# A hybrid decoder block on one core: another order of half-block products, a merge by quarters, a fixed ACT order in the FFN pairs and interleaved w_out tiles

## Chip, cores, metric

The kernel runs on one core of a Trainium2 chip. The metric is the device time of one execution in microseconds (us). Engines are named as the profile names them: PE is TensorE's matmul queue, PEld its weight loads, DVE is VectorE, ACT is ScalarE, POOL is GpSimd, SP is the queue that issues most DMAs.

## What is computed

The reference is one decoder block of width 1024 over a sequence of 1024 tokens: a Mamba-2 mixer and an RG-LRU mixer side by side, gated and merged, then a SwiGLU FFN of hidden width 2816.

```
hn = rmsnorm(h, norm1_w)
gates, z, xbc, dt, lru_x, lru_y = split(hn @ w_in)
gates = sigmoid(gates + b_branch_gate);  g_ssm, g_lru = split(gates)
y_ssm = mamba2_mixer(z, xbc, dt, ...) @ w_out_ssm
y_lru = rglru_mixer(lru_x, lru_y, ...) @ w_out_lru
h = h + (g_ssm * y_ssm + g_lru * y_lru) @ w_out
hn = rmsnorm(h, norm2_w)
gate, up = split(hn @ w_ffn_in)
h = h + (silu(gate) * up) @ w_ffn_out
return rmsnorm(h, norm_f_w)
```

## The kernel before

All data are fp32. A matrix product is made of three passes: every operand is split into a high part (a cast on ACT, L98) and a low part (a subtraction on DVE, L99), and `product` (L905 to L907) issues hi·hi, low weight·hi and hi weight·low activation for every 128 × 128 block of weights against 512 columns. In the trace a cast reads as `whi<-raw` or `xph<-xr`, its low part as `wlo` or `xpl`.

In order of time of the profiled execution: the input projections with the SSM scan (to about 770 us), the RG-LRU (to 1043), two stages for w_out_ssm (1043 to 1212), a short direct part and a third stage for w_out_lru (to 1319), w_out (to 1416), the FFN's 22 pairs (to 1927), two stages for w_ffn_out (to about 2080) and the rest with the last norm.

**Seven products.** Each of the stages is a call of `seven`: a 2 × 2 block product by seven half-size products N1 to N7 instead of eight. Its plan is a table of slots: `at(slot, f, ...)` enters weight loads, activation loads (`load_xop`), casts (`x_part`, `w_part`), weight sums (`w_sum`, on POOL: L959, L962) and products, and the events of a slot are written out in turn. Every N takes two slots, g = 0 and 1, of two products of 12 matmuls each. Before, the order is N2, N5, N3, N1, N6, N7, N4, with one bank for each of the four pairs of rows p that is carried from N2 on. The weights of (0,1), which N2 needs, come into the `raw` tile of the weight pool; the others come into `wr` units. s1 is the sum of (1,0) and (1,1), N5's weight.

**Merge.** The third stage calls `merged` after each product. After N6 the whole tile d, after N7 and N4 halves, are merged: yo = (gate + 1) · yo (L1077), res = res + yo (L1078), both on DVE, and then the halves are cast for w_out (`act_pair`, tiles `un`).

**w_out.** 16 tiles, two halves of the columns by eight row blocks d, in the order of `wo_order` (L136). After a tile of the second half with d of 4 to 7 one half tile of `bn` is cast (b22); after d of 0 to 3, `t_parts` makes four differences on DVE (L1165 to L1168) and casts two units `xth`, `xtl`.

**FFN pairs.** `first_pair` and 21 calls of `pair` make gate and up for 128 columns of hidden width by seven products: a11·b11, s1·t1, s2·t2, a12·b21, s3·t3, s4·b22, a22·t4. ACT copies banks out after the first three (L1259, L1262, L1265). The products with s2 and s3 share one bank. Between the products the next pair is made ready: loads of its two weight tiles `raw`, the split of the first (`whi`, `wlo`), four sums on POOL (L1145 to L1148, in place in `raw`), the split of s1 (`ws1h`) and of both `raw` tiles (`wsh`, `wsl`). `finish_pair` scales, applies Silu (L1214) and stores. In 8 of the pairs `pump` also makes the differences `tu` of finished tiles for w_ffn_out.

The Tile scheduler sets each engine's order by its own estimate of when things are ready, unless `pin` ties an instruction to the one pinned before it on the same engine. All loads and stores go through SP's one queue.

Of the kernel before, what the change touches and what calls it, by code (L numbers as in the profile page):

```python
# [67 lines left out]
def hybrid_block(ctx, tc, xT, w_in, w_dt, w_os, w_ol, w_o, w_fi, w_fo, w_fl, lru_w, params, heads, out):  # L68
# [10 lines left out]
    def store(dst, src):  # L79
        nc.sync.dma_start(out=dst, in_=src)  # L80
# [14 lines left out]

    def split(hi, lo, src):

        S.copy(hi, src)  # L98
        V.tensor_tensor(lo, src, hi.bitcast(F32), op=ALU.subtract)  # L99

    def split_scaled(hi, lo, src, col):

# [30 lines left out]
    order += [PJ_GATE + i for i in range(16 - last_gates, 16)]  # L133
    wseq = [(w_in[f], KD) for f in order]
    wseq_in = len(wseq)
    wo_order = [list(range(KD)), [4, 5, 6, 7, 0, 1, 2, 3]]  # L136
    wseq += [(w_o[d], KD) for h in range(2) for d in wo_order[h]]
    wseq_out = len(wseq)
    wready = []
# [172 lines left out]
    with ExitStack() as st1:  # L312
# [474 lines left out]
        with tc.tile_pool(name="lru", bufs=1, reuse_waits="tile", side="right") as lp, tc.tile_pool(  # L787
# [66 lines left out]
            def gate_done(i):  # L854
                def done(ps):
                    gt = lp.tile([P, T], F32, name="gl")
                    S.activation(gt, ps, AF.Tanh, bias=hgb[:, i : i + 1], scale=0.5)
                    store(gate_d[i], gt)

                return done  # L860

# [12 lines left out]
    def bank():  # L874
        return pb.tile([P, H], F32, name="pbk", tag="pbk")
# [44 lines left out]
    def seven(c0_, act, tdf, w_of, out, pools=None, xpool=None, swap=False, done=None):  # L922


        pools = pools or {}
        wr, wop, xr_, xop, banks = {}, {}, {}, {}, [None] * 4

        def load_w(q, kh, g):

            if (q, kh) == (0, 1):  # L930
                t_ = wpool.tile([P, KD, P], F32, name="raw", tag="raw", bufs=2)
                t_ = t_.rearrange("p (a k) c -> p a k c", a=2)
            else:
                t_ = unit(pools.get((q, kh), ar), F32, "wr").rearrange("p a (k c) -> p a k c", c=P)
            for a in range(2):
                load(t_[:, a], w_of(q * 4 + 2 * g + a, kh))
            wr[q, kh, g] = t_

        def load_xop(n, kk):

            u = unit(xpool if xpool and n == N2 else ar, F32, "xr")
            src, o, h = {
                N2: (act, 4, 0), N5: (tdf, 0, 0), N3: (act, 4, 1), N1: (act, 0, 0),
                N6: (tdf, 4, 1), N7: (tdf, 0, 1), N4: (tdf, 4, 0),
            }[n]
            if swap and src is act:
                h = 1 - h
            for a in range(2):
                load(u[:, a], src[o + 2 * kk + a][:, hcol[h]])
            xr_[n, kk] = u  # L950

        def x_part(n, kk):
            hi, lo = (unit(xpool if xpool and n == N2 else ar, name=x) for x in ("xph", "xpl"))
            split(row(hi), row(lo), row(xr_.pop((n, kk))))
            xop.setdefault(n, []).extend((hi[:, a], lo[:, a]) for a in range(2))

        def w_sum(n, g):
            w = lambda q, kh: wr[q, kh, g]
            sub = lambda o, a, b: G.tensor_tensor(o, a, b, op=ALU.subtract)  # L959
            if n == 1:  # L960
                wr["s1", g] = unit(pools.get("s1", ar), F32, "ws").rearrange("p a (k c) -> p a k c", c=P)
                G.tensor_tensor(wr["s1", g], w(1, 0), w(1, 1), op=ALU.add)  # L962
            elif n == 2:
                sub(wr["s1", g], wr["s1", g], w(0, 0))
            elif n == 3:
                sub(w(1, 0), w(0, 0), w(1, 0))
            else:
                sub(w(0, 1), w(0, 1), wr["s1", g])

        def w_part(n, g):  # L970
            key = {N2: (0, 1), N5: ("s1",), N3: (0, 1), N1: (0, 0), N6: ("s1",), N7: (1, 0), N4: (1, 1)}[n]
            hi, lo = (wpool.tile([P, 2, 4, P], F32R, name=x, tag=x) for x in ("whi", "wlo"))
            split(hi, lo, wr[(*key, g)])
            wop[n, g] = hi, lo

        def products(n, g):
            first, last = n in (N2, N5, N1), n in (N2, N3, N4)
            q, h = {N2: (0, 0), N5: (1, 1), N3: (0, 1), N1: (0, 0), N6: (0, 1), N7: (1, 1), N4: (1, 0)}[n]
            hi, lo = wop.pop((n, g))
            for a in range(2):  # L980
                p = 2 * g + a
                if first:
                    banks[p] = bank()
                product(banks[p], (hi[:, a], lo[:, a]), xop[n], first, last)
                d = q * 4 + p
                r, new = out(d, 1 - h if swap else h)
                if new and n in (N2, N5, N3, N4):
                    S.copy(r, banks[p])
                else:
                    V.tensor_tensor(r, r, banks[p], op=ALU.add)  # L990
                if done:
                    done(n, d)

        for g in range(2):
            at(c0_ - 4 + g, load_w, 0, 1, g)
            at(c0_ - 3 + g, load_w, 1, 0, g)
            at(c0_ - 3 + g, load_w, 1, 1, g)
            at(c0_ - 2 + g, load_w, 0, 0, g)
            for n in range(7):
                at(c0_ + 2 * n - 4 + g, load_xop, n, g)  # L1000
                at(c0_ + 2 * n - 2 + g, x_part, n, g)
                at(c0_ + 2 * n + g - 1, w_part, n, g)
                at(c0_ + 2 * n + g, products, n, g)
            at(c0_ + g, w_sum, 1, g)
            at(c0_ + 1 + g, w_sum, 2, g)
            at(c0_ + 2 + g, w_sum, 4, g)
            at(c0_ + 5 + g, w_sum, 3, g)
        rank = {f: r for r, f in enumerate((load_w, load_xop, w_part, x_part, w_sum, products))}
        for s in events:
            events[s].sort(key=lambda e: rank.get(e[0], 0 if e[0] not in later else 9))  # L1010
# [57 lines left out]

    mg = [[None] * KD for _ in range(2)]

    def merge(d, h=None):

        if d not in gl_t:
            gl_t[d] = load_gate(8 + d)
        v = row if h is None else (lambda t_: t_[:, h, :])
        r, y = v(res[d]), v(yo[d])
        V.scalar_tensor_tensor(y, v(gl_t[d]), 1.0, y, op0=ALU.add, op1=ALU.mult)  # L1077
        V.tensor_tensor(r, r, y, op=ALU.add)  # L1078
        for i in range(2):
            if h in (None, i):  # L1080
                mg[i][d] = act_pair(ar, res[d][:, i, :])

    gl_t = {}

    def merged(n, d):
        if n == N6:
            merge(d)
        elif n == N7:
            merge(d, 0)
        elif n == N4:  # L1090
            merge(d, 1)
# [42 lines left out]
    def pair_a1(n):  # L1134
        hi = wpool.tile([P, KD, P], F32R, name="whi", tag="whi")
        lo = wpool.tile([P, KD, P], F32R, name="wlo", tag="wlo")
        split(hi, lo, raws[n][0])
        wops[n] = {"a11": (hi[:, 0:4, :], lo[:, 0:4, :]), "a12": (hi[:, 4:8, :], lo[:, 4:8, :])}

    def pair_sums(n):  # L1140
# [8 lines left out]

    def pair_s1(n):  # L1150
        hi, lo = (sp1.tile([P, H], F32R, name=x, tag="ws1") for x in ("ws1h", "ws1l"))
        split(hi, lo, wops[n].pop("raw1"))
        wops[n]["s1"] = blk(hi), blk(lo)

    def pair_s(n, q):

        hi, lo = unit(wq, name="wsh"), unit(wq, name="wsl")
        split(row(hi), row(lo), raws[n][q].rearrange("p k c -> p (k c)"))
        for i, name in enumerate((("s2", "s4"), ("s3", "a22"))[q]):
            wops[n][name] = blk(hi[:, i, :]), blk(lo[:, i, :])  # L1160

# [49 lines left out]

    def finish_pair(j, c0, c1):
        V.tensor_tensor(row(c0), row(c0), row(rs2u), op=ALU.mult)
        S.activation(row(c0), row(c0), AF.Silu)  # L1214
        V.tensor_tensor(c1[:, 1, :], c1[:, 1, :], rs2[1], op=ALU.mult)
        V.tensor_tensor(row(c0), row(c0), row(c1), op=ALU.mult)
        store(act_d[j], row(c0))
# [31 lines left out]
    def pair(n, nxt, pump):  # L1249
# [6 lines left out]
        prep(pair_load)  # L1256
        pu, pv, px = bank(), bank(), bank()
        product(pu, wo["a11"], x["b11"], True, False)
        S.copy(c0[:, 0, :], pu)  # L1259
        pump()  # L1260
        product(pv, wo["s1"], x["t1"], True, False)
        S.copy(c1[:, 1, :], pv)  # L1262
        pump()
        product(pu, wo["s2"], x["t2"], False, False)
        S.copy(c0[:, 1, :], pu)  # L1265
        prep(pair_a1)
        pump()
        product(px, wo["a12"], x["b21"], True, True)
# [229 lines left out]
```

## Time and profile before

| what | value |
|---|---|
| median of 3 runs | 2174.2 us (2172.35 to 2176.2) |
| the profiled execution | 2175.62 us |
| its span | 2173.9 us |
| PE busy | 2061.8 us (95%), 9506 matmuls |
| DVE busy | 1401.4 us (64%) |
| ACT busy | 934.4 us (43%) |
| POOL busy | 516.4 us (24%) |
| mean granted clock of TensorE | 0.972 |

The span is the time between the first and the last instruction; 1.7 us of the execution lie around it. A granted clock of 1.00 is 2.4 GHz, 0.50 is 1.2 GHz. A line such as `PE pbk L905 <- ACT c L1265: 44.8, 19, 3.5` says that PE's matmuls of line 905 waited for ACT's instruction of line 1265 for 44.8 us in 19 waits, the longest 3.5.

### The profile page before, as it was taken

What the parts mean: (1) busy time and instruction counts of PE and PEld (TensorE: products, weight loads), DVE (VectorE), ACT (ScalarE), POOL (GpSimd) and SP (SyncE); (2) the same over time, 40 slices, a digit from 0 to 9 for tenths busy, and PEclk for the clock granted to TensorE, in tenths of its full rate; (3) what the DMA queues carried; (4) which work ended last, traced back from release to release, by engine and by line L of the source; (5) the groups of instructions that cost most, each with busy time, mean ns of one, the idle gap of its engine ahead of it and who ended that gap; (6) DMA issues with size and microseconds to landing.
All of it is one profiled execution on the core that took longest, in us unless ns stands there. A gap on an engine that the chain in (4) does not pass through costs nothing. (4 is left out here: it accounts for less than half of the span.)

```text
span 2173.9 us, 24882 instructions
## 1 busy us (share of the span) xinstructions
PE 2061.8 (95%) x9506; PEld 1664.6 (77%) x9506; DVE 1401.4 (64%) x1626; ACT 934.4 (43%) x1291; POOL 516.4 (24%) x414
## 2 busy tenths in 40 slices
PE   8999999999999999999799998989889899889998
PEld 6678887887878888888688877867677677668888
DVE  8665666667667467576568687684555455469745
ACT  5334454455454356666443433542223223224334
POOL 5113333334333300000422311242222222241200
PEclk8999999999999999999899999999999999989999
DMA  3313224223224275253555433522332243276212
GB/s 136 97 57 95 82 64 140 74 76 130 80 76 133 76 267 204 88 200 126 198 198 182 147 98 114 182 83 78 128 135 96 88 148 133 73 261 216 66 52 89
DMA packets 120615, 269.85 MB, mean 124 GB/s; under 512 B 13488, under 2 KB 32944, under 8 KB 120496
## 3 DMA queue, kind: packets, MB, share of 16 engines
q1 hardware_dynamic: 120496, 268.27, 36.8%
q8 instruction: 74, 1.21, 0.2%
q14 instruction: 45, 0.37, 0.0%
HBM read 205.04 MB, written 63.18 MB: 123 GB/s over the span
## 5 line engine op out<-in xcount | busy, mean ns | idle before, releaser
L173 PE MATMUL pj<-hnh,whi 128*128 128x512 f32 x1152 | 461.1, 400 | 0.0
L175 PE MATMUL pj<-hnl,whi 128*128 128x512 f32 x1152 | 452.9, 393 | 0.0
L174 PE MATMUL pj<-hnh,wlo 128*128 128x512 f32 x1152 | 452.3, 393 | 0.0
L175 PEld LDWEIGHTS pj<-hnl,whi 128*128 128x128 f32 x1152 | 216.6, 188 | 48.1 <-issue 0.5
L173 PEld LDWEIGHTS pj<-hnh,whi 128*128 128x128 f32 x1152 | 216.7, 188 | 46.0 <-issue 2.4
L174 PEld LDWEIGHTS pj<-hnh,wlo 128*128 128x128 f32 x1152 | 217.0, 188 | 45.0 <-issue 1.4
L905 PE MATMUL pbk<-xph,whi 128*128 128x512 f32 x560 | 221.1, 396 | 13.4 <-ACT whi L98 10.2
L906 PE MATMUL pbk<-xph,wlo 128*128 128x512 f32 x560 | 221.8, 396 | 6.0 <-DVE wlo L99 6.0
L907 PE MATMUL pbk<-xpl,whi 128*128 128x512 f32 x560 | 220.4, 396 | 6.4 <-DVE xpl L99 6.3
L99 DVE TENSOR_TENSOR wlo<-raw,whi 128x1024 fp32r<-128x1024 f32 (+1 forms) x138 | 181.2, 1314 | 52.4 <-ACT whi L98 52.3
L98 ACT CAST whi<-raw 128x1024 fp32r<-128x1024 f32 (+1 forms) x138 | 142.5, 1033 | 96.6 <-PE pbk L175 32.0
L905 PE MATMUL pbk<-xth,wsh 128*128 128x512 f32 x264 | 115.2, 436 | 45.4 <-ACT c L1265 44.8
L98 ACT CAST wsh<-raw 128x1024 fp32r<-128x1024 f32 x44 | 45.9, 1048 | 226.0 <-issue 137.0
L905 PEld LDWEIGHTS pbk<-xph,whi 128*128 128x128 f32 x560 | 107.0, 191 | 37.7 <-ACT whi L98 11.0
L962 POOL TENSOR_TENSOR ws<-wr 128x1024 f32<-128x1024 f32 x10 | 28.6, 2856 | 442.2 <-DMA wr<-in_w_os 299.3
L907 PEld LDWEIGHTS pbk<-xpl,whi 128*128 128x128 f32 x560 | 107.2, 191 | 31.3 <-DVE xpl L99 9.2
L906 PEld LDWEIGHTS pbk<-xph,wlo 128*128 128x128 f32 x560 | 106.9, 191 | 30.5 <-DVE wlo L99 7.9
L644 ACT ACTIVATE E<-csb,cs 128x128 f32<-128x128 f32 x256 | 82.8, 392 | 108.1 <-PE yb L685 101.0
L99 DVE TENSOR_TENSOR xpl<-xr,xph 128x1024 fp32r<-128x1024 f32 x70 | 113.4, 1626 | 24.1 <-ACT xph L98 19.2
L98 ACT CAST xph<-xr 128x1024 fp32r<-128x1024 f32 x70 | 72.7, 1049 | 97.4 <-DVE xpl L99 53.5
L907 PE MATMUL pbk<-xtl,wsh 128*128 128x512 f32 x264 | 113.4, 430 | 0.6 <-DVE xtl L99 0.6
L1145 POOL TENSOR_TENSOR ws<-raw 128x512 f32<-128x512 f32 x22 | 30.0, 1363 | 350.3 <-DMA raw<-in_w_fi 314.7
(303 smaller groups left out, 4198.3 us busy)
## 6 DMA issues: line engine op xcount, KB each, us to landing
raw<-in_w_in SPq DMA_DIRECT2D x74, 512.0 KB, 3.5
raw<-in_w_fi SPq DMA_DIRECT2D x44, 512.0 KB, 3.5
csb<-cs_d SPq DMA_DIRECT2D x64, 256.0 KB, 3.5
act_d<-c SPq DMA_DIRECT2D x22, 512.0 KB, 4.0
yn_d<-xs SPq DMA_DIRECT2D x16, 512.0 KB, 3.3
tu<-yn_d SPq DMA_DIRECT2D x16, 512.0 KB, 6.7
ty_d<-tu SPq DMA_DIRECT2D x16, 512.0 KB, 4.1
xr<-ty_d SPq DMA_DIRECT2D x32, 256.0 KB, 4.1
```

The source lines that it names most:

```text
L98: S.copy(hi, src)
L99: V.tensor_tensor(lo, src, hi.bitcast(F32), op=ALU.subtract)
L173: PE.matmul(ps, wh, xh, start=i == 0, stop=False)
L174: PE.matmul(ps, wl, xh, start=False, stop=False)
L175: PE.matmul(ps, wh, xl, start=False, stop=i == n - 1)
L644: S.activation(E[:, j, :], csb[:, j, :], AF.Relu, bias=cs[:, c, h0 + j : h0 + j + 1], scale=-1.0)
L905: PE.matmul(ps, wh, xh, start=first and k == 0, stop=False, skip_group_check=True)
L906: PE.matmul(ps, wl, xh, start=False, stop=False, skip_group_check=True)
L907: PE.matmul(ps, wh, xl, start=False, stop=last and k == n - 1, skip_group_check=True)
L962: G.tensor_tensor(wr["s1", g], w(1, 0), w(1, 1), op=ALU.add)
L1145: G.tensor_tensor(blk(s1), u_[:, 0:4, :], u_[:, 4:8, :], op=ALU.add)
```

## The change

- `seven` runs N1, N2, N5, N3, N6, N7, N4. Each pair p has three banks: u for N1, N6, N7 and N4, x for N2, v for N5 and N3. Weight (0,0) takes the `raw` tile, (0,1) a `wr` unit. The four POOL sums stay, in other slots: s1 at the first slot after the start, two sums one later, the last one later again; s1 less (0,0) is put into the place of (0,0).
- The merge runs by quarters, one half of one tile, after N2, N6, N7 and N4. The half of the gate is loaded into a buffer `gt` of its own, the multiply stays on DVE, the add is POOL's.
- `split` hands back ACT's instruction, and from the FFN on every cast, bank copy and Silu of ACT is pinned in the order in which the program writes them.
- The second half of w_out takes its tiles in the order 4, 0, 5, 1, 6, 2, 7, 3.
- The stores of the last two gate tiles are issued by ACT instead of SP.
- The out stages use another choice of pools.

Line numbers of the changed kernel differ: up to about L1066 they are one higher than before, in the pairs nine lower.

```diff
@@ split
-        S.copy(hi, src)
+        ins = S.copy(hi, src)
         V.tensor_tensor(lo, src, hi.bitcast(F32), op=ALU.subtract)
+        return ins
@@ 
-    wo_order = [list(range(KD)), [4, 5, 6, 7, 0, 1, 2, 3]]
+    wo_order = [list(range(KD)), [4, 0, 5, 1, 6, 2, 7, 3]]
@@ last gate tiles
-                    store(gate_d[i], gt)
+                    S.dma_start(out=gate_d[i], in_=gt)
@@ seven
-    N2, N5, N3, N1, N6, N7, N4 = range(7)
+    N1, N2, N5, N3, N6, N7, N4 = range(7)
...
-            if (q, kh) == (0, 1):
+            if (q, kh) == (0, 0):
...
             elif n == 2:
-                sub(wr["s1", g], wr["s1", g], w(0, 0))
-            elif n == 3:
                 sub(w(1, 0), w(0, 0), w(1, 0))
+                sub(w(0, 0), wr["s1", g], w(0, 0))
             else:
-                sub(w(0, 1), w(0, 1), wr["s1", g])
+                sub(w(0, 1), w(0, 1), w(0, 0))
...
-            first, last = n in (N2, N5, N1), n in (N2, N3, N4)
+            first, last = n in (N1, N2, N5), n in (N2, N3, N4)
...
+                b = "x" if n == N2 else "v" if n in (N5, N3) else "u", p
                 if first:
-                    banks[p] = bank()
+                    banks[b] = bank()
...
-            at(c0_ - 4 + g, load_w, 0, 1, g)
-            at(c0_ - 3 + g, load_w, 1, 0, g)
-            at(c0_ - 3 + g, load_w, 1, 1, g)
-            at(c0_ - 2 + g, load_w, 0, 0, g)
+            at(c0_ - 4 + g, load_w, 0, 0, g)
+            at(c0_ - 3 + g, load_w, 0, 1, g)
+            at(c0_ - 2 + g, load_w, 1, 0, g)
+            at(c0_ - 2 + g, load_w, 1, 1, g)
...
-            at(c0_ + g, w_sum, 1, g)
-            at(c0_ + 1 + g, w_sum, 2, g)
-            at(c0_ + 2 + g, w_sum, 4, g)
-            at(c0_ + 5 + g, w_sum, 3, g)
+            for n in range(1, 4):
+                at(c0_ + n + g, w_sum, n, g)
@@ merge
-    def merge(d, h=None):
...
-        V.scalar_tensor_tensor(y, v(gl_t[d]), 1.0, y, op0=ALU.add, op1=ALU.mult)
-        V.tensor_tensor(r, r, y, op=ALU.add)
...
+    def merge(d, h):
+        gt = temp2("gt")
+        load(gt, gate_d[8 + d][:, hcol[h]])
+        r, y = res[d][:, h, :], yo[d][:, h, :]
+        V.scalar_tensor_tensor(y, gt, 1.0, y, op0=ALU.add, op1=ALU.mult)
+        G.tensor_tensor(r, r, y, op=ALU.add)
+        mg[h][d] = act_pair(ar, r)
...
+        if n in (N2, N6, N7, N4):
+            merge(d, int(n in (N2, N4)))
@@ FFN
+    pinned.clear()
+    order = pin
...
-        split(hi, lo, raws[n][0])
+        order(split(hi, lo, raws[n][0]))
...
-        S.activation(row(c0), row(c0), AF.Silu)
+        order(S.activation(row(c0), row(c0), AF.Silu))
...
-        S.copy(c0[:, 0, :], pu)
+        order(S.copy(c0[:, 0, :], pu))
...
-        S.copy(c1[:, 1, :], pv)
+        order(S.copy(c1[:, 1, :], pv))
...
-        S.copy(c0[:, 1, :], pu)
+        order(S.copy(c0[:, 1, :], pu))
```

Three places in the order of instructions follow.

ACT in one pair of the FFN, before; `c` is the pair's output, copied from a bank, L1265 the third copy, L1214 Silu:

```order
L98 CAST whi<-raw 128x1024
L1259 COPY c_11462<-pbk 128x512
L1262 COPY c_11463<-pbk 128x512
L98 CAST ws1h<-ws_11526 128x512
L98 CAST wsh<-raw 128x1024
L1265 COPY c_11462<-pbk 128x512
L98 CAST wsh<-raw 128x1024
L1214 ACTIVATE c_11462<-c_11462 128x1024
```

ACT in one pair of the FFN, after; the three copies are L1250, L1253 and L1256 there, Silu L1205:

```order
L1250 COPY c_11486<-pbk 128x512
L1253 COPY c_11487<-pbk 128x512
L1256 COPY c_11486<-pbk 128x512
L98 CAST whi<-raw 128x1024
L98 CAST ws1h<-ws_11550 128x512
L98 CAST wsh<-raw 128x1024 x2
L1205 ACTIVATE c_11486<-c_11486 128x1024
```

The third copy has moved ahead of the casts ws1h and wsh, and the cast of whi behind the copies.

ACT at the start of the first stage of seven products, before; `gl` is a gate tile, `res<-pbk` the copies of the first N, `whi<-ws` the cast of a weight sum:

```order
L98 CAST whi<-raw 128x1024
L98 CAST dxh<-dx 128x1024
L988 COPY res<-pbk 128x512 x4
L98 CAST xph<-xr 128x1024 x2
L98 CAST whi<-ws 128x1024
L98 CAST xph<-xr 128x1024
```

The same place after:

```order
L859 DMA gate_d_135<-gl 128x1024
L98 CAST dxh<-dx 128x1024
L989 COPY res<-pbk 128x512 x2
L98 CAST whi<-wr 128x1024
L989 COPY res<-pbk 128x512 x2
L98 CAST whi<-wr 128x1024
L98 CAST xph<-xr 128x1024 x5
L98 CAST whi<-ws 128x1024
```

Between the first N's copies and the first weight sum, the casts of a second raw weight and of more activations have come in; ACT issues the gate's store.

DVE in the second half of w_out, before; `bn` rows are the differences of `t_parts`, `r<-pbk` ends a tile:

```order
L1165 TENSOR_TENSOR bn<-bn 128x512
L1166 TENSOR_TENSOR bn<-bn 128x512
L1167 TENSOR_TENSOR bn<-bn 128x512
L1194 SCALAR_TENSOR_TENSOR r<-pbk,r 128x512
L1168 TENSOR_TENSOR bn<-bn 128x512
L99 TENSOR_TENSOR xtl<-bn,xth 128x1024
L99 TENSOR_TENSOR wlo<-raw,whi 128x1024
L99 TENSOR_TENSOR xtl<-bn,xth 128x1024
L1165 TENSOR_TENSOR bn<-bn 128x512
```

The same place after, where `un<-bn` is the split of a b22 tile and the differences are L1156 to L1159:

```order
L1159 TENSOR_TENSOR bn<-bn 128x512
L99 TENSOR_TENSOR xtl<-bn,xth 128x1024
L1185 SCALAR_TENSOR_TENSOR r<-pbk,r 128x512
L99 TENSOR_TENSOR xtl<-bn,xth 128x1024
L99 TENSOR_TENSOR wlo<-raw,whi 128x1024
L99 TENSOR_TENSOR un<-bn,un 128x512
L1185 SCALAR_TENSOR_TENSOR r<-pbk,r 128x512
L99 TENSOR_TENSOR wlo<-raw,whi 128x1024
L1156 TENSOR_TENSOR bn<-bn 128x512
```

Between the differences of one tile and those of the next stands now a tile without differences.

## Rows read from the trace of the kernel before

**Rows 1.** Waits of PE, whole span: engine, line, waited for, us, times, longest.

```profile
PE pbk L905 <- ACT c L1265: 44.8, 19, 3.5
PE pbk L905 <- ACT whi L98: 10.2, 2, 9.3
...
PE pbk L907 <- DVE xpl L99: 6.3, 4, 3.6
```

**Rows 2.** Stretches: length, busy us (instructions) of PE, PEld, DVE, ACT, POOL, clock, DMA.

```profile
1100.00:1200.00 100.00, 100.00 (x443) 82.81 (x442) 77.74 (x73) 38.59 (x40) 24.39 (x8) 1.00 0.56 189
...
1045.00:1095.00 50.00, 37.39 (x151) 29.36 (x150) 28.91 (x17) 23.71 (x30) 23.47 (x8) 0.86 0.70 244
1285.00:1335.00 50.00, 40.68 (x153) 31.08 (x153) 44.72 (x60) 19.31 (x29) 0.00 (x0) 0.90 0.26 88
1410.00:1447.00 37.00, 29.76 (x113) 21.79 (x114) 36.35 (x32) 18.09 (x23) 18.71 (x10) 0.95 0.20 65
1447.00:1905.00 458.00, 413.20 (x1669) 328.65 (x1668) 233.76 (x253) 128.47 (x161) 109.66 (x80) 0.94 0.32 110
1920.00:1960.00 40.00, 31.53 (x113) 23.52 (x112) 31.61 (x21) 11.39 (x12) 24.29 (x8) 0.83 0.72 256
```

**Rows 3.** Stretches again: one FFN pair with the wait, and the last pair.

```profile
1570.20:1593.50 23.30, 21.03 (x84) 16.84 (x84) 13.58 (x16) 6.39 (x8) 5.17 (x5) 0.93 0.46 158
1907.30:1926.70 19.40, 19.40 (x85) 15.78 (x84) 10.18 (x11) 5.97 (x7) 2.40 (x1) 1.00 0.91 312
```

**Rows 4.** Timeline of ACT in pairs: start, us, instruction, [idle before <-releaser].

```profile
1570.89 1.05 ACT L98 CAST wsh<-raw 128x1024 fp32r<-128x1024 f32 x1 [3.80 <-POOL raw L1148]
1571.84 0.58 ACT L1265 COPY c<-pbk 128x512 f32<-128x512 f32 x1
...
1582.88 1.06 ACT L1214 ACTIVATE c<-c 128x1024 f32<-128x1024 f32 x1 [1.86 <-DVE c L1213]
...
1910.24 0.59 ACT L1259 COPY c<-pbk 128x512 f32<-128x512 f32 x1
...
1915.76 0.59 ACT L1265 COPY c<-pbk 128x512 f32<-128x512 f32 x1 [2.21 <-PE pbk L907]
```

**Rows 5.** Timeline of POOL, the last two pair sums ahead of that cast.

```profile
1567.89 1.62 POOL L1147 TENSOR_TENSOR raw<-ws,raw 128x512 f32<-128x512 f32 x1
1569.58 1.27 POOL L1148 TENSOR_TENSOR raw<-raw 128x512 f32<-128x512 f32 x1
```

**Rows 6.** Timelines of DVE and POOL in the first seven: alone, then beside each other.

```profile
1065.28 1.21 DVE L99 TENSOR_TENSOR wlo<-ws,whi 128x1024 fp32r<-128x1024 f32 x1
...
1067.55 3.38 DVE L99 TENSOR_TENSOR wlo<-ws,whi 128x1024 fp32r<-128x1024 f32 x1
...
1056.34 2.34 POOL L959 TENSOR_TENSOR wr<-wr 128x1024 f32<-128x1024 f32 x1
...
1066.58 3.28 POOL L959 TENSOR_TENSOR ws<-ws,wr 128x1024 f32<-128x1024 f32 x1 [2.30 <-DVE wlo L99]
```

**Rows 7.** Timeline of DVE in a pair with `tu` work.

```profile
1569.95 1.45 DVE L301 TENSOR_TENSOR tu<-tu 128x512 f32<-128x512 f32 x1 [1.60 <-DMA tu<-act_d]
```

**Rows 8.** Timeline of SP's queue (issues) at the first seven products.

```profile
1040.92 0.32 SPq L77 DMA_DIRECT2D dx<-yl_d  x1
1044.66 0.32 SPq L80 DMA_DIRECT2D gate_d<-gl  x1
1045.02 5.46 SPq L77 DMA_DIRECT2D wr<-in_w_os  x10
```

**Rows 9.** Groups of DVE instructions, 1282 to 1329 us: count, busy us, mean ns.

```profile
L1078 DVE TENSOR_TENSOR res<-res,yo 128x512 f32<-128x512 f32 (+1 forms) x12 | 10.2, 865 | 0.0
```

**Rows 10.** Timeline of DVE at the end of w_out.

```profile
1409.79 0.68 DVE L1165 TENSOR_TENSOR bn<-bn 128x512 f32<-128x512 f32 x1
...
1413.04 1.22 DVE L99 TENSOR_TENSOR xtl<-bn,xth 128x1024 fp32r<-128x1024 f32 x1
```

More of the change, by code (lines that the diff above doesn't have):

```diff
@@ L925, in seven @@
         pools = pools or {}
-        wr, wop, xr_, xop, banks = {}, {}, {}, {}, [None] * 4
+        wr, wop, xr_, xop, banks = {}, {}, {}, {}, {}
         def load_w(q, kh, g):
-            if (q, kh) == (0, 1):
+            if (q, kh) == (0, 0):
                 t_ = wpool.tile([P, KD, P], F32, name="raw", tag="raw", bufs=2)
@@ L939, in load_xop @@
         def load_xop(n, kk):
-            u = unit(xpool if xpool and n == N2 else ar, F32, "xr")
+            u = unit(xpool if xpool and n == N1 else ar, F32, "xr")
             src, o, h = {
@@ L952, in x_part @@
         def x_part(n, kk):
-            hi, lo = (unit(xpool if xpool and n == N2 else ar, name=x) for x in ("xph", "xpl"))
+            hi, lo = (unit(xpool if xpool and n == N1 else ar, name=x) for x in ("xph", "xpl"))
             split(row(hi), row(lo), row(xr_.pop((n, kk))))
@@ L963, in w_sum @@
             elif n == 2:
-                sub(wr["s1", g], wr["s1", g], w(0, 0))
-            elif n == 3:
                 sub(w(1, 0), w(0, 0), w(1, 0))
+                sub(w(0, 0), wr["s1", g], w(0, 0))
             else:
-                sub(w(0, 1), w(0, 1), wr["s1", g])
+                sub(w(0, 1), w(0, 1), w(0, 0))
         def w_part(n, g):
-            key = {N2: (0, 1), N5: ("s1",), N3: (0, 1), N1: (0, 0), N6: ("s1",), N7: (1, 0), N4: (1, 1)}[n]
+            key = {N2: (0, 1), N5: ("s1",), N3: (0, 1), N1: (0, 0), N6: (0, 0), N7: (1, 0), N4: (1, 1)}[n]
             hi, lo = (wpool.tile([P, 2, 4, P], F32R, name=x, tag=x) for x in ("whi", "wlo"))
@@ L981, in products @@
                 p = 2 * g + a
+                b = "x" if n == N2 else "v" if n in (N5, N3) else "u", p
                 if first:
-                    banks[p] = bank()
-                product(banks[p], (hi[:, a], lo[:, a]), xop[n], first, last)
+                    banks[b] = bank()
+                product(banks[b], (hi[:, a], lo[:, a]), xop[n], first, last)
                 d = q * 4 + p
                 r, new = out(d, 1 - h if swap else h)
-                if new and n in (N2, N5, N3, N4):
-                    S.copy(r, banks[p])
+                if new and n in (N1, N5, N3, N4):
+                    S.copy(r, banks[b])
                 else:
-                    V.tensor_tensor(r, r, banks[p], op=ALU.add)
+                    V.tensor_tensor(r, r, banks[b], op=ALU.add)
                 if done:
@@ L1069, in hybrid_block @@
     mg = [[None] * KD for _ in range(2)]
-    def merge(d, h=None):
[L1073 to L1076, printed above, removed]
-        V.scalar_tensor_tensor(y, v(gl_t[d]), 1.0, y, op0=ALU.add, op1=ALU.mult)
-        V.tensor_tensor(r, r, y, op=ALU.add)
[L1079 to L1083, printed above, removed]
-    def merged(n, d):
[L1086 to L1091, printed above, removed]
+    def merge(d, h):
[5 more added lines that the diff above has]
+        mg[h][d] = act_pair(ar, r)
+    def merged(n, d):
+        if n in (N2, N6, N7, N4):
+            merge(d, int(n in (N2, N4)))
     DIR = 2 * CYC
@@ L1151, in pair_s1 @@
         hi, lo = (sp1.tile([P, H], F32R, name=x, tag="ws1") for x in ("ws1h", "ws1l"))
-        split(hi, lo, wops[n].pop("raw1"))
+        order(split(hi, lo, wops[n].pop("raw1")))
         wops[n]["s1"] = blk(hi), blk(lo)
@@ L1157, in pair_s @@
         hi, lo = unit(wq, name="wsh"), unit(wq, name="wsl")
-        split(row(hi), row(lo), raws[n][q].rearrange("p k c -> p (k c)"))
+        order(split(row(hi), row(lo), raws[n][q].rearrange("p k c -> p (k c)")))
         for i, name in enumerate((("s2", "s4"), ("s3", "a22"))[q]):
@@ L1299, in hybrid_block @@
             lambda d, h: (res[d][:, h, :], False),
-            pools={"s1": wq, **({(0, 0): ar0} if i == 0 else {k: ar0 for k in ((0, 0), (1, 0), (1, 1))})},
+            pools={"s1": wq, **({(1, 0): ar0} if i == 0 else {k: ar0 for k in ((0, 1), (1, 0), (1, 1))})},
         )
```

## Prediction

> **What bounds the kernel now.** I read the waits of TensorE first [rows 1], since TensorE is the engine that the end hangs on, then a table of stretches with the busy time and granted clock of each [rows 2], and then the timelines of the stretches that stand out. A stretch where TensorE is fed sets the price of a matmul: 443 of them in 100.00 us, 0.2257 us each, at a granted clock of 1.00, which is the 2.4 GHz level. What any other stretch loses is its length less its matmuls at that price: 50.00 − 151 × 0.2257 = 15.9 us around the start of the first seven-product stage, 50.00 − 153 × 0.2257 = 15.5 around the merge, 37.00 − 113 × 0.2257 = 11.5 between w_out and the FFN, 40.00 − 113 × 0.2257 = 14.5 between the FFN and its output product [rows 2]. In the long stretch of FFN pairs the wait list names one thing, TensorE's hi·hi matmul waiting for ACT's copy of L1265: 44.8 us in 19 waits of at most 3.5 [rows 1]. The clock there is 0.94 on average, while the one pair that never waits holds 1.00 [rows 2, 3]. So the kernel is TensorE's, and what can be won is these five places.
>
> **FFN pairs: ACT's order.** The copy of L1265 empties the bank into which the product with s3 goes. Its data are there before it runs: on ACT the cast of wsh stands ahead of it, and that cast waited 3.80 us for POOL's last sum (1569.58 + 1.27 = 1570.85, cast at 1570.89, copy only at 1571.84) [rows 4, 5]. The change pins the copies ahead of the casts, as the order of ACT above shows. The copy then follows its product directly, as in the pair without a wait (1915.76, 2.21 after ACT had become free, on TensorE's release) [rows 4]. Between its release and its need lies one product of 12 matmuls, 2.7 us, and the copy takes 0.6: some 2 us are spare, so the wait goes and not only a part of it. Its price is read twice. By waits and clock: 44.8, and (1 − 0.94) × 458 = 27.5 for matmuls run at a lower clock, together 72.3 [rows 1, 2]. By period: a pair with the wait takes 23.30, the one without 19.40, and 19 × 3.90 = 74.1 [rows 3]. I take 73.
>
> What the pin adds: the cast of whi, so far ahead of the next pair's first copy, now stands behind the third. From that copy the chain is whi 1.05, wlo 1.21, POOL's L1147 1.62 and L1148 1.27, two casts of wsh at 1.05, Silu 1.06: 8.3 us, with wlo alone as in [rows 6]. From third copy to the next pair's first there are 19.40 − (1915.76 − 1910.24) = 13.9 [rows 4, 5]. The two POOL sums queue behind wlo now; nothing else is on POOL there. Behind them on ACT stand only the wsh casts and Silu, whose products come a pair later. With wlo at 3.38 and both sums at 2.3 (an estimate, as far stretched as the 1024-wide sum of [rows 6], and more) the chain is 12.2, still inside. In the 8 pairs with the extra `tu` work DVE runs closer: a `tu` difference of 512 columns took 1.45 beside POOL [rows 7], where one as wide takes 0.68 alone [rows 10], 0.8 each, so 0 to 6 us for the eight; I charge 1, since the chain has room. Term: −72, bounds −74 and −66.
>
> **Start of the first seven products.** Before, four N2 products run and then TensorE stands 9.3 us [rows 1] for the cast of `ws`, a weight sum that POOL makes from loads that SP could issue only from 1045.02, behind a gate store at 1044.66 that waited for its tanh [rows 8]; SP issued nothing between dx at 1040.92 and that store. Now N1 comes first and N2 second, both on raw weights; the sum is due 24 matmuls × 0.2257 × 2 slots = 10.8 us later. The gate store goes to ACT's queue, where it waits for nothing that ACT has not just made, at the price of two issues there (0.32 each, by SP's); the loads can start at about the end of the store ahead of them, up to 3.7 us sooner (1045.02 less 1040.92 + 0.32, when the load of dx is out [rows 8]). So this wait should go. What is late next: ACT must cast the x of N2 (two casts of 1.05 and DVE's two 1.21) behind N1's four copies, whose last ends when N1 ends, so N2 opens some 3 us late; and N5's wlo and xpl run beside POOL's sums. DVE's wlo takes 1.21 alone and 3.38 beside a sum, and a sum 2.34 alone and 3.28 beside DVE: 1.21 + 2.34 = 3.55, nearly the two in turn [rows 6]. Eight sums, as before, four of them earlier. Loss left: 5 (the N2 opening and its slow matmuls) to 17 (every low part of N2 and N5 behind a sum). Nearest is the middle, since N5's wlo is the one that comes beside sums either way: about 10. Term −6, bounds −11 and +1.
>
> **Merge.** DVE is busy 44.72 of 50 us here, TensorE 40.68 [rows 2]; DVE's lateness reaches w_out's first wlo. The adds of L1078 (10.2 us in 12 instructions) go to POOL as 16 adds of 512 columns, and 4 of 16 half-tile gate multiplies move forward to N2 [rows 9]. Without contention DVE loses about 10.2 + 4 × 0.68 = 12.9 us, which would clear most of the 15.5. POOL's adds read and write the same tiles: 1.27 us each, by L1148 [rows 5]. Were each to hold DVE up for its length, the 12 in the last three products cost 15.2 and DVE is as late as before. No row shows a 512-wide add beside this DVE stream; [rows 6] is the nearest and shows near-full serialisation for work that does meet. But POOL's adds are short, and DVE's adds out of banks (L990) read a bank and one tile, where both operands of the stretched row are tiles. Each add also puts POOL's hop between the DVE multiply and ACT's cast. I take −4, bounds −10 and +3.
>
> The Trainium skill speaks against this edit. "SBUF — State Buffer", section "Who interferes with whom", states that a DVE instruction with two SBUF inputs contends with a GpSimd instruction that reads SBUF, whoever is first holding the shared pair for the whole instruction. By it the merge term is +3 and not −4, and the trace agrees as far as 3.38 against 1.21 goes [rows 6]. Rival B is that rule carried to all starts.
>
> **w_out to FFN.** A tile of the second half with the four differences (L1165 to L1168) costs DVE 4 × 0.68 + 2 × 1.22 + 0.68 + 1.21 = 7.1 us, against 24 × 0.2257 = 5.4 on TensorE; four such tiles stood last, in a row, with POOL's first pair sums beside them [rows 10]. Now each stands beside a light one (0.68 + 1.21 + 0.69 = 2.6; the pair 9.7 against 10.8), so no backlog of 4 × 1.7 = 6.8 builds up, and only the last heavy tile meets the sums. Of the 11.5 lost here I take −7, bounds −11 (all) and 0 (the last tile alone holds it).
>
> **FFN to its output product.** N1 first on data long loaded helps, but the four early sums on POOL meet the casts of N1 and N2. TensorE waits 6.3 for xpl [rows 1], within a loss of 14.5. I take 0, bounds −6 and +4. The second seven-product stage runs at 1.00 already; three banks a pair and the ACT-issued stores cost nothing there, since TensorE never waits.
>
> **Sum.** −72 − 6 − 4 − 7 + 0 = −89. The profiled execution is 2175.6, so 2086.6; the median of the runs is 1.4 below it, so 2085.
>
> **Rivals.**
> A, the forecast: 2085, own range 2072 to 2100. Chance 0.68.
> B, POOL and DVE in turn: the pair waits go, but every start is as bad as its upper bound: −66 + 1 + 3 + 0 + 4 = −58, so 2116. For it: [rows 6]. Against: at w_out nothing new meets POOL. 0.12.
> C, all five places clear: −74 − 15.9 − 15.5 − 11.5 − 14.5 = −131, so 2043. Against it, N2's casts behind N1's copies and POOL's sums remain. 0.10.
> D, the copies come in time but the clock stays at 0.94, for small gaps stay in each pair: −45 − 10 = −55, so 2119. Against: one pair without a wait has 1.00 [rows 3]. 0.04.
> E, slower: ACT's pinned order becomes the loop. A wsh cast waiting for POOL's sums now blocks Silu and the next pair's copies too. With the other terms at −17, the total rises above the old time by 0.2% only when a pair passes 23.30 + 21/19 = 24.4 us, so the chain 24.4 − 5.5 = 18.9, against 8.3 reckoned and 12.2 stretched. At 25.0 a pair: 19 × 1.7 − 17 = +15, so 2189. 0.03.
> F, the change does not do what it says: the pin leaves a cast that waits ahead of the copy, and the starts give and take: 2174. The order on ACT speaks against it. 0.03.
>
> **How the numbers follow.** The likeliest is A, 2085. A and B hold 0.80; the range runs from 2062 (all lower bounds, −112) to 2117 (B). Faster or slower by over 0.2%, about what a measurement of this kernel can tell from no change: faster A to D, 0.94; same F, 0.03; slower E, 0.03.
>
> **What would show it.** In the changed profile: no wait for the third copy in the pairs, a period near 19.4 and a clock of 0.99 or 1.00 from 1447 us on; the 9.3 wait replaced by one of about 3 at N2; POOL adds in the merge with DVE multiplies of over 1 us beside them; no wait for xtl or wsh at the first pair. The forecast is wrong if pairs stay above 20.5 us, or if the starts lose more than the 57 us that they lose now.

## The result, and the profile after

The changed kernel takes 2101.0 us (median of 4 runs, 2100.16 to 2102.07); the kernel before took 2173.27 beside it (median of 4). The ratio is 0.9666, with a 95% interval of 0.9649 to 0.9683. The forecast was 2085 in a range of 2062 to 2117: the direction and the main term held, 16 us of the 89 expected did not come, and the time lies 1 us above the 2072 to 2100 that the prediction gave its own case, A.

The page of the changed kernel, busy time and share of the span of each engine:

```profile
PE 2036.4 (97%) x9506; PEld 1648.4 (78%) x9506; DVE 1395.7 (66%) x1618; ACT 934.6 (45%) x1291; POOL 538.0 (26%) x430
```

TensorE's busy time fell from 2061.8 to 2036.4 with the same 9506 matmuls: they ran at the full clock more often (mean granted clock 0.983, before 0.972). The stretches of the changed kernel, with the columns of [rows 2]; the fourth begins and ends inside the FFN pairs, the fifth is a single pair:

```profile
1045.00:1095.00 50.00, 40.41 (x156) 31.19 (x155) 36.42 (x23) 23.13 (x28) 23.53 (x8) 0.86 0.61 205
...
1285.00:1335.00 50.00, 44.42 (x188) 34.54 (x188) 44.73 (x49) 21.22 (x29) 19.27 (x13) 1.00 0.33 109
...
1410.00:1447.00 37.00, 28.55 (x98) 20.84 (x97) 29.10 (x23) 14.49 (x19) 17.06 (x9) 0.86 0.18 63
...
1447.00:1832.00 385.00, 384.74 (x1662) 311.70 (x1661) 222.95 (x249) 125.79 (x159) 112.73 (x80) 1.00 0.37 129
...
1832.00:1851.30 19.30, 19.30 (x85) 15.72 (x84) 10.34 (x11) 7.02 (x8) 0.00 (x0) 1.00 0.76 258
```

In the pairs the clock is 1.00 and TensorE is busy 384.74 of 385.00 us, where it was busy 413.20 of 458.00 at 0.94. The first seven loses 50.00 − 156 × 0.2257 = 14.8 us, against 15.9. Between w_out and the second pair only 98 matmuls ran in 37 us, against 113: that stretch got worse. The waits of TensorE that are left, over the whole span (engine, line, waited for: us, times, longest):

```profile
PE pbk L906 <- ACT xph L98: 10.3, 5, 3.9
PE pbk L908 <- DVE xpl L99: 10.1, 8, 2.2
PE pbk L907 <- DVE wlo L99: 4.6, 5, 1.4
PE pbk L906 <- DVE c L1228: 4.6, 1, 4.6
```

The 44.8 us of [rows 1] are gone. What is left are mostly waits for the splits of activations and weights. One wait has grown, that for L1228, an add of the first FFN pair, from 0.6 us to 4.6. In the kernel before it is the line

```profile
PE pbk L905 <- DVE c L1237: 0.6, 1, 0.6
```

To see where the time went, the start of the k-th matmul is compared in both traces. Both programs run 9506, and the stages have the same counts, so the difference between two such indices is what a stage won or lost. One execution of each kernel is compared, and stages that no edit touches differ by up to 3 us from trace to trace, so a difference of that size in one stage proves little. In us, against the kernel before:

| stage (matmul numbers) | forecast | after |
|---|---|---|
| first seven (5000 to 5250) | −6 | −1.1 |
| third seven with the merge (5700 to 6200) | −4 | −3.2 |
| w_out to the second pair (6200 to 6650) | −7 | +5.2 |
| FFN pairs (6650 to 8360) | −72 | −71.3 |
| FFN to its output product (8360 to 8500) | 0 | −3.4 |
| all else | 0 | +0.1 |
| sum | −89 | −73.7 |

### The profile page after: what moved, and what is told of

It is laid out like the page before. It is cut to its first block, busy times and chain, and to the rows that moved or that the text cites. A ratio compares the mean times of both kernels' runs of the same rounds, so it can differ in the third digit from the quotient of the medians.

```text
span 2100.1 us, 24937 instructions
## 1 busy us (share of the span) xinstructions
PE 2036.4 (97%) x9506; PEld 1648.4 (78%) x9506; DVE 1395.7 (66%) x1618; ACT 934.6 (45%) x1291; POOL 538.0 (26%) x430
## 5 line engine op out<-in xcount | busy, mean ns | idle before, releaser
L99 DVE TENSOR_TENSOR wlo<-raw,whi 128x1024 fp32r<-128x1024 f32 (+1 forms) x138 | 188.4, 1366 | 186.5 <-ACT whi L98 186.3
L175 PEld LDWEIGHTS pj<-hnh,wlo 128*128 128x128 f32 x1152 | 217.2, 189 | 44.8 <-issue 1.4
L99 DVE TENSOR_TENSOR xpl<-xr,xph 128x1024 fp32r<-128x1024 f32 x70 | 108.3, 1555 | 15.4 <-ACT xph L98 12.8
L906 PE MATMUL pbk<-xth,wsh 128*128 128x512 f32 x264 | 107.1, 406 | 4.8 <-DVE c L1228 4.6
L907 PE MATMUL pbk<-xth,wsl 128*128 128x512 f32 x264 | 106.0, 401 | 0.0
L908 PE MATMUL pbk<-xtl,wsh 128*128 128x512 f32 x264 | 106.0, 401 | 0.0
```

Source lines behind the costliest of these rows:

```text
L175: PE.matmul(ps, wl, xh, start=False, stop=False)
L906: PE.matmul(ps, wh, xh, start=first and k == 0, stop=False, skip_group_check=True)
L907: PE.matmul(ps, wl, xh, start=False, stop=False, skip_group_check=True)
L908: PE.matmul(ps, wh, xl, start=False, stop=last and k == n - 1, skip_group_check=True)
```

## Experiments

Each kernel was timed beside the kernel before. Ratios are to that kernel; the changed kernel has 0.9666 (0.9649 to 0.9683).

**The pin alone.** The kernel before with the ACT order of the FFN pairs fixed and nothing else. (The section on the change says that from the FFN on every cast, bank copy and Silu is pinned; the diff pins the splits of the pairs' weights, Silu, and the copies of `pair`. The three copies of `first_pair` and the casts of activations are not pinned, which matters below.)

```diff
+    pinned.clear()
+    order = pin
...
-        split(hi, lo, raws[n][0])
+        order(split(hi, lo, raws[n][0]))
...
-        S.copy(c0[:, 1, :], pu)
+        order(S.copy(c0[:, 1, :], pu))
```

(and the same for the other splits, copies and Silu of the pairs)

> The kernel before with nothing but the pinned ACT order in the FFN. Theory: the pin alone is the whole gain of the FFN pairs, which between the first matmul of the second pair and the last of pair 21 was 71.3 us in the changed kernel; all other edits together gave about 2. So 2173 - 71 = 2102, no wait for the third copy, clock 1.00 in the pairs, and the stretch from w_out to the second pair as before (it lost 11.5 us). Rival 1: the pin needs the other edits (data that arrive earlier), then only part of the waits goes: 2115 to 2145. Rival 2: the pin itself caused the 4.6 us wait for L1228 in the first pair; then it is seen here too and the time is 2107.

Measured: 2101.6 us, ratio 0.9678 (0.9663 to 0.9693). The pairs gained 71.3, every other stage between −0.8 and +0.6. The stretch of the pairs in this kernel, columns as before:

```profile
1447.00:1832.00 385.00, 384.74 (x1661) 311.67 (x1660) 225.10 (x251) 126.60 (x159) 112.76 (x80) 1.00 0.38 131
```

It reads as that of the changed kernel. One edit makes the whole of the measured gain, as far as the times can tell. The wait for the add of the first pair (L1240 here) is 0.6 us, as in the kernel before, so rival 2 of this run falls too. Which of the pinned instructions count was not tried apart.

**Everything but the pin.** The changed kernel with

```diff
-    order = pin
+    order = lambda ins: ins
```

> The changed kernel with the ACT order of the FFN left to the scheduler. Theory: the pair waits come back whole (19 of about 2.4 us and a clock of 0.94): 2101 + 71 = 2172, so that all other edits together are worth 1 to 3 us. In the first pair the cast of wsh still stands ahead of copy L1224 and the 4.6 us wait stays, since the pin is not its cause. Rival: the wait in the first pair goes with the pin, 2166.

Measured: 2169.95 us, ratio 0.9985 (0.9975 to 0.9995). All other edits together are worth 0.15%, some 3 us. The pair waits are back:

```profile
PE pbk L906 <- ACT c L1256: 42.5, 19, 3.1
```

The wait of 4.6 us for L1228 is there too, so it is not the pin's doing. ACT in the first pair (start, us, instruction, [idle before]):

```profile
1428.67 0.58 ACT L1220 COPY c<-pbk 128x512 f32<-128x512 f32 x1
1434.27 1.04 ACT L98 CAST wsh<-raw 128x1024 fp32r<-128x1024 f32 x1 [5.02 <-POOL raw L1139]
1435.22 0.58 ACT L1224 COPY c<-pbk 128x512 f32<-128x512 f32 x1
```

The cast waits 5.02 us for POOL, and the copy of a bank stands behind it: the pattern of [rows 4], once, in `first_pair`, whose copies the change does not pin.

**The first pair's copies pinned.** The changed kernel with

```diff
-        S.copy(c0[:, 0, :], pu)
-        S.copy(c0[:, 1, :], pv)
+        order(S.copy(c0[:, 0, :], pu))
+        order(S.copy(c0[:, 1, :], pv))
...
-        S.copy(c1[:, 1, :], pw)
+        order(S.copy(c1[:, 1, :], pw))
```

> The changed kernel with the three bank copies of the first pair pinned too. Theory: the cast of wsh for pair 1, which waits 5.0 us for POOL's sums, stood ahead of the copy L1224 and caused the 4.6 us wait for L1228 and some 2 us at the lower clock behind it; with the copy ahead both go: 2101 - 6 = 2095. Rival: the casts and their low parts are late anyhow for the second pair (wsl, ws1l behind POOL's stretched sums), and TensorE waits there instead: 2099 to 2101.

Measured: 2096.39 us, ratio 0.9652 (0.9637 to 0.9667). By the traces w_out to the second pair is at −2.4 against before, where it was at +5.2. The wait for L1228 falls from 4.6 to 0.9 us. The copy now runs before the casts of the next pair, and the stretch holds 131 matmuls in place of 98:

```profile
1427.71 0.58 ACT L1224 COPY c<-pbk 128x512 f32<-128x512 f32 x1
...
1434.11 0.62 ACT L98 CAST ws1h<-ws 128x512 fp32r<-128x512 f32 x1 [2.73 <-POOL ws L1136]
1438.55 2.00 ACT L98 CAST wsh<-raw 128x1024 fp32r<-128x1024 f32 x2 [3.82 <-POOL raw L1139]
```

```profile
1410.00:1447.00 37.00, 32.11 (x131) 23.82 (x131) 28.06 (x26) 15.80 (x22) 14.16 (x10) 1.00 0.24 80
```

**The old order of the w_out tiles.** The changed kernel with

```diff
-    wo_order = [list(range(KD)), [4, 0, 5, 1, 6, 2, 7, 3]]
+    wo_order = [list(range(KD)), [4, 5, 6, 7, 0, 1, 2, 3]]
```

> The changed kernel with the w_out tiles of the second half in the old order. Theory: it was the interleaved order that let the scheduler put the copy L1224 behind the cast of wsh (in the build with the pin alone and in this one the copy stands ahead); with the old order the 4.6 us wait is gone and the stretch is as in the kernel before: 2101 - 5 = 2096. Rival: the backlog of DVE returns as the prediction reckoned it (7 us): 2104 to 2108.

Measured: 2100.66 us, ratio 0.9648 (0.9621 to 0.9675); its time cannot be told from the changed kernel's, and the 2096 that was expected did not come. Its trace differs: the stage is at 0.0 against before, where the changed kernel has +5.2, and there is no wait for L1228. ACT copies as soon as the product is done:

```profile
1430.18 0.59 ACT L1224 COPY c<-pbk 128x512 f32<-128x512 f32 x1 [1.90 <-PE pbk L908]
```

So it is the interleaved order that made the scheduler place the cast ahead. What the stage won here, this execution lost again on code that is the same in both: at the FFN's output (−0.1, where the changed kernel has −3.4) and in the first seven (+0.8 against −1.1). Together with the run before: the interleave is worth some 2.4 us once the copy is in its place (−2.4 against 0.0), not 7. This compares one trace of each, and the pinned copies are a second difference between them.

**Gate stores on SP.** The changed kernel with

```diff
-                    S.dma_start(out=gate_d[i], in_=gt)
+                    store(gate_d[i], gt)
```

> The changed kernel with the last two gate stores back on SP's queue. Theory: the store that ACT issues at 1044.4 us holds SP's loads up (its run of eight weight loads took 11.31 us to issue, where ten took 5.46 before), so the x of N2 lands late (ACT waited 4.2 us for it); with the store on SP the loads start at 1045.0 and run on, and N2 opens no later: 2098 to 2101. Rival, the step of the prediction: the store on ACT lets the loads start 3.7 us sooner, and taking it back costs that and the lower clock: 2104 to 2107.

Measured: 2099.9 us, ratio 0.9671 (0.9654 to 0.9688): no difference from the changed kernel that the runs can tell. The rival's 2104 to 2107 falls. The issues of SP, first in the changed kernel, then here, show why the earlier start of the loads was worth nothing:

```profile
1041.09 11.31 SPq L77 DMA_DIRECT2D wr<-in_w_os  x8
1052.45 0.91 SPq L77 DMA_DIRECT2D xr<-yn_d  x2
```

```profile
1044.23 4.35 SPq L77 DMA_DIRECT2D wr<-in_w_os  x8
1048.63 1.70 SPq L77 DMA_DIRECT2D xr<-yn_d  x2
```

With the store on ACT the run of eight loads begins 3.1 us sooner and takes 11.31 us instead of 4.35, so the next loads come 3.8 us later. The waits of SP's queue between 1035 and 1056 us put this down to the landing of the gate store:

```profile
SPq L77 <- DMA gate_d<-gl: 6.7, 1, 6.7
```

With the store on SP there is no such wait. Why SP's loads wait for a store that they do not read is not shown. By the traces the store on ACT even costs a little: the first seven stands at −1.9 here, and at −1.8 in both combinations below, against −1.1 to +0.8 in the five kernels with the store on ACT and the same code in this stage. That is about 1 us, too little for the times to show.

**N2's activations first.** The changed kernel with

```diff
-            at(c0_ - 2 + g, load_w, 1, 0, g)
-            at(c0_ - 2 + g, load_w, 1, 1, g)
+            at(c0_ - 1 + g, load_w, 1, 0, g)
+            at(c0_ - 1 + g, load_w, 1, 1, g)
...
-        rank = {f: r for r, f in enumerate((load_w, load_xop, w_part, x_part, w_sum, products))}
+        rank = {f: r for r, f in enumerate((load_xop, load_w, w_part, x_part, w_sum, products))}
```

> The changed kernel with SP's loads in another order at each stage: the x of N2 ahead of the weights (1,0) and (1,1), which are loaded one slot later. Theory: at the first stage TensorE waits 3.9 and 1.7 us for ACT's casts of N2's x, and ACT waited 4.2 us for that x to land behind 2 MB of weights that only N5 needs; with x first these two waits and some of the lower clock go: 2101 - 5 = 2096. Rival, POOL and DVE in turn: N2 opens in time but N5 then waits for wlo and xpl beside POOL's sums, which now start later: 2100 to 2104.

Measured: 2102.4 us, ratio 0.966 (0.964 to 0.968). The rival holds. N2 opens after a wait of 2.56 us instead of 3.92, the later waits of N2 are 0.72 in place of 0.76, 1.68 and 2.23, and N5 pays them back in one piece. TensorE in this kernel:

```profile
1056.51 0.50 PE L906 MATMUL pbk<-xph,whi 128*128 128x512 f32 x1 [2.56 <-ACT xph L98]
1057.96 0.80 PE L908 MATMUL pbk<-xpl,whi 128*128 128x512 f32 x1 [0.72 <-DVE xpl L99]
1075.89 0.80 PE L907 MATMUL pbk<-xph,wlo 128*128 128x512 f32 x1 [4.14 <-DVE wlo L99]
```

**Fewer sums beside DVE.** The changed kernel with six of the eight sums of the first seven left out, so that N3, N6, N7 and N4 multiply by weights that are not the sums:

```diff
+            if xpool and n > 1:
+                return
```

> The changed kernel with six of the eight POOL sums of the first seven-product stage left out, so that this stage computes with wrong weights for N3, N6, N7 and N4; matmuls, casts and loads are the same. It prices POOL beside DVE there. Theory (taking turns): TensorE's waits for xpl and wlo at the start come from DVE's splits stretched from 1.22 to about 3.4 us beside the sums; without the six the splits are short and the stage's start, which loses 15 us, loses about 9: 2095. Rival: the loads set the start (N2's x and the weights land late) and it stays: 2099 to 2101.

Measured: 2095.43 us, ratio 0.9626 (0.9613 to 0.9639). In the first seven the waits for xpl and wlo are gone and those for xph are left. Waits of TensorE from 1040 to 1100 us, in the changed kernel and then here:

```profile
PE pbk L906 <- ACT xph L98: 5.6, 2, 3.9
PE pbk L908 <- DVE xpl L99: 3.0, 2, 2.2
PE pbk L907 <- DVE wlo L99: 1.0, 1, 1.0
```

```profile
PE pbk L906 <- ACT xph L98: 6.4, 2, 5.2
```

```profile
1045.00:1095.00 50.00, 43.55 (x169) 33.88 (x168) 27.67 (x24) 24.97 (x29) 5.08 (x2) 0.86 0.67 231
```

The loss is 50.00 − 169 × 0.2257 = 11.9 us in place of 14.8. By the start of matmuls the stage stands at −4.3, the changed kernel at −1.1. So about three of the fifteen are POOL beside DVE; what is left in the wait list is N2's x, and the clock of the stretch is still 0.86. I had expected six of the fifteen: a miss by half. That the time of 2095.43 met the 2095 expected is luck: of the 8 us by which the two traces differ the stage holds 3, the rest lies in stages whose code is the same.

**The merge's adds on DVE.** The changed kernel with

```diff
-        G.tensor_tensor(r, r, y, op=ALU.add)
+        V.tensor_tensor(r, r, y, op=ALU.add)
```

> The changed kernel with the 16 quarter adds of the merge on DVE instead of POOL. In the changed trace the merge stretch gained 3.2 us against before; beside POOL's adds a 512-wide DVE split takes 1.77 us for 0.69 alone, and ACT's casts wait 3.5 to 5.7 us for an add and stand ahead of the x casts that TensorE waits for. Theory (taking turns): what DVE gives to POOL it loses again in stretched instructions and in the hop, so the time is the same, 2099 to 2103. Rival 1, as the prediction had it: the hand-over is worth several us, and without it the loss of before returns: 2104 to 2108. Rival 2: the hop alone is what is left of the loss: 2095 to 2098.

Measured: 2097.34 us, ratio 0.9638 (0.962 to 0.9656), its median 3.7 us below the changed kernel's with intervals that overlap. By the traces the merge stage is at −6.3 against before, the changed kernel at −3.2; the other kernels with the adds on POOL stand between −0.5 and −4.2, the second one with the adds on DVE, below, at −5.1. DVE's instructions from 1240 to 1335 us (count, busy us, mean ns), in the changed kernel and then here:

```profile
L99 DVE TENSOR_TENSOR un<-res,un 128x512 fp32r<-128x512 f32 x16 | 16.3, 1025 | 7.3 <-ACT un L98 6.8
L1074 DVE SCALAR_TENSOR_TENSOR yo<-gt,yo 128x512 f32<-128x512 f32 x16 | 13.9, 880 | 0.2
...
L99 DVE TENSOR_TENSOR wlo<-raw,whi 128x1024 fp32r<-128x1024 f32 x6 | 9.5, 1585 | 1.1 <-ACT whi L98 1.1
```

```profile
L1074 DVE SCALAR_TENSOR_TENSOR yo<-gt,yo 128x512 f32<-128x512 f32 x16 | 12.0, 762 | 0.1
...
L99 DVE TENSOR_TENSOR un<-res,un 128x512 fp32r<-128x512 f32 x16 | 10.8, 684 | 0.3
L1075 DVE TENSOR_TENSOR res<-res,yo 128x512 f32<-128x512 f32 x16 | 10.8, 683 | 0.1
...
L99 DVE TENSOR_TENSOR wlo<-raw,whi 128x1024 fp32r<-128x1024 f32 x6 | 7.3, 1218 | 1.2 <-ACT whi L98 1.2
```

DVE takes over 10.8 us of adds and gets back 5.5 + 1.9 + 2.2 = 9.6 from these three groups, which ran longer in the kernel with POOL's adds: the hand-over gave DVE almost nothing. In the changed kernel it also stood idle 6.8 us for ACT's `un` casts, which wait for POOL. ACT at one such place there:

```profile
1292.01 0.62 ACT L98 CAST un<-res 128x512 fp32r<-128x512 f32 x1 [3.51 <-POOL res L1075]
1292.53 1.04 ACT L98 CAST xph<-xr 128x1024 fp32r<-128x1024 f32 x1
```

The `xph` cast that TensorE needs stands behind a cast that waits for POOL's add. The run without POOL in the merge gives that idle time back. What the merge gained over the kernel before must then come from the rest of its edits, the quarters that start at N2 or the new order of the products; these were not tried apart.

**Combinations.** The first pair's copies, the gate stores on SP and N2's activations first, together:

> The changed kernel with the first pair's copies pinned, the gate stores on SP and x loaded first. If the gains add: -5 (first pair) - 1 (stores) - 5 (x first) = 2090. Rival: x first gives nothing, 2095.

Measured: 2094.68 us, ratio 0.9625 (0.9604 to 0.9645), the time of the first pair's copies alone as far as the runs tell: activations first adds nothing. Then the first pair's copies, the adds on DVE and the gate stores on SP:

> The changed kernel with the three edits that were each no slower: the first pair's copies pinned, the merge's adds on DVE, the gate stores on SP. The places are apart (first seven, merge, first pair), so the gains should add: 2101 - 5 - 3 - 1 = 2092. Rival: what is won at the first pair or in the merge is taken back at the next stage, 2096.

Measured: 2089.47 us (5 runs, 2088.54 to 2094.85), ratio 0.9598 (0.9585 to 0.9612), an interval wholly below that of the changed kernel. By the trace of one execution the stages stand at −1.8 (first seven), −5.1 (merge), −2.6 (to the second pair), −71.8 (pairs) and 0.0 (to the output product). That execution, 2094.85, is the slowest of the five, so the median has gains that it does not show. This version beats both kernels.

## Why the prediction was right or wrong

**FFN pairs: right in mechanism and size** (−72 forecast, −71.3 measured, and by the pin alone). ACT in a pair of the changed kernel shows the steps, then one sum of POOL:

```profile
1571.42 0.59 ACT L1256 COPY c<-pbk 128x512 f32<-128x512 f32 x1 [2.21 <-PE pbk L908]
1571.90 1.05 ACT L98 CAST whi<-raw 128x1024 fp32r<-128x1024 f32 x1
1572.85 0.62 ACT L98 CAST ws1h<-ws 128x512 fp32r<-128x512 f32 x1
1577.70 1.05 ACT L98 CAST wsh<-raw 128x1024 fp32r<-128x1024 f32 x1 [4.23 <-POOL raw L1139]
1579.81 1.05 ACT L98 CAST wsh<-raw 128x1024 fp32r<-128x1024 f32 x1 [1.06 <-PE pbk L908]
1583.29 1.06 ACT L1205 ACTIVATE c<-c 128x1024 f32<-128x1024 f32 x1 [2.43 <-DVE c L1204]
1585.43 0.59 ACT L1250 COPY c<-pbk 128x512 f32<-128x512 f32 x1 [1.08 <-PE pbk L908]
...
1574.36 1.61 POOL L1138 TENSOR_TENSOR raw<-ws,raw 128x512 f32<-128x512 f32 x1 [2.65 <-DVE wlo L99]
```

The copy is released by TensorE alone. The cast of wsh still waits 4.23 us for POOL, whose L1138 now waits for the later wlo, but what stands behind it is not due. The second wsh cast ends 9.4 us after the third copy began and Silu 12.9, in the 14.0 to the next pair's first copy. The 8.3 that was reckoned to the end of Silu was too short: it left out that the second wsh cast is held by TensorE (1.06) and Silu by DVE's scaling (2.43). Still the next copy is released by TensorE, 1.08 after ACT had become free, so rival E did not come about, and the lateness charged for the `tu` pairs (0 to 6, taken as 1) cost nothing to be seen: TensorE is busy 384.74 of 385.00 us. Both prices, by waits with clock and by period, held; rival D fell with the clock of 1.00.

**w_out to FFN: wrong, by 12 us and in sign** (−7 forecast, +5.2 measured). The step that failed is "only the last heavy tile meets the sums". It looked at DVE alone. The order of ACT in the first pair was not gone through: with interleaved tiles a cast of wsh stands ahead of the copy L1224, the very defect that the change removes in the other pairs. DVE's add L1225 waits for that copy, L1228 stands behind it on DVE, and TensorE waits for L1228. DVE and TensorE in the changed kernel:

```profile
1436.22 0.69 DVE L1225 TENSOR_TENSOR c<-c,pbk 128x512 f32<-128x512 f32 x1 [2.73 <-ACT c L1224]
...
1437.96 0.68 DVE L1228 TENSOR_TENSOR c<-c,pbk 128x512 f32<-128x512 f32 x1
...
1438.70 0.79 PE L906 MATMUL pbk<-xth,wsh 128*128 128x512 f32 x1 [4.56 <-DVE c L1228]
```

With the copies pinned the wait is 0.9, with the old tile order there is none. The term itself was too large as well: without the defect the interleave is worth some 2.4, not 7. TensorE's waits between 1395 and 1447 us sum to 6.6 with the old order and to 5.9 with the new one and the copies pinned, so the order of the tiles alone moved little of it. DVE's splits are long there in the changed kernel too: `wlo` took 2.30 us at 1410.98 and 1427.29, the second beside a pair sum of POOL.

**First seven: the direction held, the size not** (−6 forecast, −1.1 measured, inside the bounds). The 9.3 us wait for the sum went, and N2 opened 3.92 late, where some 3 was said. Too small was the loss left: 14.8, not 10. Two things were not in the sum. The step on the gate store had the loads start some 3.7 us sooner; they do start at 1041.09, but then SP waits 6.7 us for the store that ACT issued, which by the run with that store on SP costs about 1 us. And N2's x lands behind the weights in either case: ACT waited 4.20 us for a load before the second of its casts.

```profile
1056.94 1.04 ACT L98 CAST xph<-xr 128x1024 fp32r<-128x1024 f32 x1 [1.18 <-DMA xr<-yn_d]
1062.18 1.04 ACT L98 CAST xph<-xr 128x1024 fp32r<-128x1024 f32 x1 [4.20 <-DMA xr<-yn_d]
```

The forecast put the lateness of N2 on ACT's four copies. The run with N2's activations first shows what is theirs: with x landed in time N2 still opens 2.56 late, so the loads added 1.4 there, and more behind it; but loading x first only moved the wait to N5. That DVE's splits are stretched beside POOL's sums held too (two xpl took 6.73 us from 1063.26), and by the run with few sums it costs about 3 us here.

**Merge: the size was right by luck** (−4 forecast, −3.2 measured). The step that failed is the gain of the hand-over: the adds on POOL were to leave DVE a net gain, and by the run with the adds on DVE they left none. The Trainium skill's rule ("SBUF — State Buffer", section "Who interferes with whom") on two-input DVE instructions and GpSimd reads agrees with the rows: a `un` split took 1.025 us on average in the kernel with POOL's adds and 0.684 in the one without. It did not give the sign of the term: the other edits of the stage, which stand at −6.3 without POOL, more than paid for it. Rival B priced the rule at +3 here and the sum at 2116; the loss it stands for is real, only smaller than what the other parts of the edits brought.

**FFN to its output product** (0 forecast, −3.4 measured): inside the bounds of −6 and +4. Kernels with the same code there stand between 0.0 and −4.7, without a pattern that their edits explain, so how much of it is the new order stays open. The kernel with the pin alone stands at −0.8 on the code of before.

The sum: −89 forecast, −73.7 by the traces. Of the 15 us between them 12 lie between w_out and the second pair, 5 in the first seven and some 1 each in the merge and the pairs, less 3 gained at the output product.

## What to carry to other kernels

Do not put an instruction that waits for a slow producer ahead of one that frees a bank on the same engine: here the third copy stood behind such a cast in 19 pairs, which cost 71 us in waits and lower clock, and pinning the order of one engine took them back. After any edit of an order, walk the whole order of every engine whose waits count, also at the edges (the first pair here), for the same pattern. Work handed from DVE to POOL was almost no gain here, where DVE's other instructions on two tiles ran at the same time. In such a place price it as if the two took turns, and add the hop.

## What the runs showed of the hardware

The 16 adds handed to POOL were almost paid in full by DVE, as 9.6 us of longer instructions against 10.8 us of adds, though most of POOL's adds last only 1.29 us (1.48 on average). And SP's issue of eight loads took 11.31 us with ACT issuing a store in between, against 4.35 with that store in SP's own queue; 6.7 us of it SP waited for that store to land, by the wait list. Why it waits for it was not tried apart.
